# The down product of a gated FFN: eleven pairs by seven products instead of nine pairs and a plain rest

## The chip, the core and the metric

The kernel runs on one core of one Trainium2 chip. The core has a matrix engine (TensorE, "PE" in the profile, its weight loads "PEld"), a vector engine (VectorE, "DVE"), a scalar engine (ScalarE, "ACT"), a general engine (GpSimd, "POOL") and a queue engine (SyncE, "SP") that issues most DMAs; the engines run at the same time and wait for each other by semaphores. The metric is the time of one execution in microseconds (us) on the device.

## The reference

The program is a two-layer decoder trunk on 512 tokens of width 1024, all in float32. Layer 0 has a state-space mixer, layer 1 multi-head latent attention; each is followed by a layer norm, a gated FFN and a second layer norm. The change concerns the FFN:

```python
def conv_ffn(h, up, conv_w, conv_b, down):
    u = causal_depthwise_conv(h @ up, conv_w, conv_b)
    g, val = jnp.split(u, 2, axis=-1)
    return (jax.nn.silu(g) * val) @ down
...
ff = conv_ffn(h, ffn_up[i], ffn_conv_w[i], ffn_conv_b[i], ffn_down[i])
h = layer_norm(DN_ALPHA * h + ff, ln_ffn_g[i], ln_ffn_b[i])
```

The hidden width is 2816, which is 22 hidden tiles of 128. FFN 0 is followed by the attention's down projection, FFN 1 by the output.

## The kernel before, in words

**Precision.** Every float32 operand of a product is split into a high part (rounded to the matmul format by ACT) and a low part (the difference, by DVE). A product is three matmuls: high times high, high times low, low times high (`mm_b`). One matmul has a 128x128 stationary tile and 512 moving columns.

**The weight stream (`WStream`).** All weights of the program are a list of items in the order of use. `load` brings an item into a staging tile `wst` (SP's queue), `_split` makes its high and low parts `wh` and `wl` (ACT line 96, DVE line 97). There are six buffers of `wh` and of `wl`; `ahead` splits items until these are taken, `retire` gives a pair back when the last product has used it. Items have a kind: "r" loads into a running sum `rs`, "a" adds onto that sum by a DMA that accumulates (POOL's queue), "+" adds a staged tile onto the sum on DVE (line 88), "=" is that staged tile itself, "-" is the sum minus a staged tile (DVE, line 91), no kind is a plain weight.

**An FFN.** In an up phase, each hidden tile takes two items (gate and value, 24 matmuls each, line 159), and `conv3_silu_gate` makes the gated tile on ACT and DVE (lines 327 to 333). Two hidden tiles make a pair: `pair_operands` builds from the even and odd tile, cut in two halves of 256 tokens, the seven left operands of a seven-multiplication scheme for 2x2 blocks (Winograd's form of Strassen's), named a11, a12, a22, s1, s2, s3, s4, and splits them into `gt` buffers (18 of them). a11 needs the even tile alone. The right operands are the sums and differences that the item kinds make, and the results are added onto the residual stream `h` by DVE (line 387). A round is an up phase and then the seven products of its pairs; the pairs are grouped into parts of two or one (a part of two has weight items of 1024 columns).

Before the change there are two rounds, with parts (2,2,1) and (2,1,1), which is nine pairs or 18 hidden tiles, and the last four hidden tiles (their up items come in the second round's up phase, after its pairs') are multiplied plainly after the second round: for each token tile of 128 both halves of 512 columns, 24 matmuls in all (`piece`, lines 165 to 167), then that tile's layer norm. `add_mix` (line 185) adds with a row sum, `ln_stats` takes the mean on DVE and the squares on ACT, `ln_var` the factor on DVE or POOL, `ln_a` (line 210) and `ln_b` (line 215) are two DVE passes of two halves. In FFN 0 the finished tiles are transposed on TensorE for the attention (`transpose_h`, lines 274 to 278), tiles 0 and 1 inside the tail and tiles 2 and 3 inside the attention's start; in FFN 1 they are written out, and the last token tile is cut in two halves of 256 columns (`ln_last`, lines 243 to 264).

**What sets the order.** A framework orders each engine's queue at build time: of the instructions whose inputs it takes to be ready, the earliest in program order goes first. So an instruction can stand in its queue well ahead of its place in the program. `issue_after(x)` ties the instructions of a block behind x on x's engine. SP's queue is ordered by hand. On the chip each engine's queue runs in that fixed order.

Of the kernel before, what the change touches and what calls it, by code (L numbers as in the profile page):

```python
# [18 lines left out]
P = 128  # L19
# [11 lines left out]
class WStream:  # L31
# [44 lines left out]
    def _split(self, nst=None):  # L76
# [17 lines left out]
        h = self.k.wh.tile([P, 1024], F32R, name="wh")  # L94
        l = self.k.wl.tile([P, 1024], F32R, name="wl")
# [16 lines left out]
    def retire(self, i):  # L112
        assert i == self.done
        del self.w[i]
        self.done += 1


class K:
# [87 lines left out]
    def ln_a(self, i, dst):  # L206

        for f in range(2):
            sl = slice(f * 512, (f + 1) * 512)
            self.nc.vector.scalar_tensor_tensor(dst[:, sl], self.h[:, i, sl], self.st[i][:, 2:3], self.gb[0][:, sl],  # L210
                                                op0=ALU.add, op1=ALU.mult)

    def ln_b(self, i, f, src):
        sl = slice(f * 512, (f + 1) * 512)
        self.ln_end = self.nc.vector.scalar_tensor_tensor(self.h[:, i, sl], src[:, sl], self.st[i][:, 5:6], self.gb[1][:, sl],
# [15 lines left out]
    def ln_last(self, i, bs, out, between):  # L231
# [19 lines left out]
        nc.vector.scalar_tensor_tensor(h3, h3, 1.0, bs[1], op0=ALU.mult, op1=ALU.add, accum_out=sb)  # L251
# [14 lines left out]
    def transpose_h(self, i):  # L266
# [3 lines left out]
        for q in range(2):  # L270
# [7 lines left out]
            nc.vector.tensor_tensor(self.htt[:, q * 4:(q + 1) * 4, 1, ts], bv, hi, op=ALU.subtract)  # L278
# [9 lines left out]
RP0 = ((2, 2, 1), (2, 1, 1))  # L288
RP1 = ((2, 2, 1), (2, 1, 1))


def rounds(rp):
    r0 = 2 * sum(rp[0])
    return r0, r0 + 2 * sum(rp[1])


def ffn_items(up, down, rp):
# [4 lines left out]
    R0, R1 = rounds(rp)  # L302
    dv = down.rearrange("(k p) n -> p k n", p=P)
    for r, ks in enumerate((range(R0), range(R0, HT))):
        for c in ks:
            it.append((up[c], 1024))
            it.append((up[c + HT], 1024))

        for odd, hf, kinds in ((0, 0, "r"), (0, 1, "a"), (1, 1, "+="), (0, 0, "-"), (1, 0, None), (1, 0, "a")):
            j = ks[0]  # L310
            for p, n in enumerate(rp[r]):
                b = dv[:, j:j + 2 * n, hf * 512:(hf + 1) * 512].rearrange("p (k e) n -> p k e n", e=2)[:, :, odd, :]
                it += [(b, n * 512, kind, p) for kind in kinds or (None,)]
# [47 lines left out]
def down_pairs(k, ws, n, prs, parts, first, between):  # L361

    nc = k.nc
    X, Y, Z = ([k.bank() for _ in range(2)] for _ in range(3))
    ni = len(parts)
    at = [sum(parts[:p]) for p in range(ni + 1)]
    new = {(i, hf) for i in range(NT) for hf in range(2)} if first else set()  # L370

    def product(bs, op, p, i, start, stop):
        wh, wl = ws.get(i, 3)
        ps = prs[at[p]:at[p + 1]]
        for t in range(2):
            for q, pr in enumerate(ps):
                x, c0 = pr[op]
                sl = slice(q * 512, (q + 1) * 512)
                k.mm_b(bs[t], x, slice(c0 + t * P, c0 + (t + 1) * P), wh[:, sl], wl[:, sl],
                       start and p == 0 and q == 0, stop and p == ni - 1 and q == len(ps) - 1)  # L380
        ws.retire(i)

    def add(bs, row, hf, sign):
        for t in range(2):
            i = 2 * row + t
            hs = k.h[:, i, hf * 512:(hf + 1) * 512]
            last = nc.vector.scalar_tensor_tensor(hs, hs, ALPHA if (i, hf) in new else 1.0, bs[t], op0=ALU.mult,  # L387
                                                  op1=ALU.add if sign > 0 else ALU.subtract)
            new.discard((i, hf))
        return last  # L390

    def ahead(n, ins):

        with k.tc.issue_after(ins.ins):
            ws.ahead(n)

    for p in range(ni):
        product(X, "a11", p, n + p, True, True)
    n += ni
    ahead(n, add(X, 0, 0, 1))  # L400
    for p in range(ni):
        product(Y, "s1", p, n + p, True, True)
    n += ni
    ahead(n, add(Y, 1, 1, 1))
    between()
    for p in range(ni):
        product(X, "s2", p, n + 2 * p, False, True)
        product(Y, "s4", p, n + 2 * p + 1, False, True)
    n += 2 * ni
    add(X, 0, 1, -1)  # L410
    ahead(n, add(Y, 0, 1, 1))
    for bs, op, s0, out in ((X, "s3", False, (1, 1, -1)), (Z, "a12", True, (0, 0, 1)), (X, "a22", False, (1, 0, 1))):
        for p in range(ni):
            product(bs, op, p, n + p, s0, True)
        n += ni
        ahead(n, add(bs, *out))
    return n


def ffn(k, ws, base, cwp, gb, rp, la=2, out=None, mid=None):  # L420

    nc, tc = k.nc, k.tc
    R0, R1 = rounds(rp)
    with ExitStack() as c:
        pool = lambda n, b: c.enter_context(tc.tile_pool(name=n, bufs=b))
        pools = {"gt": pool("gt", 18), "fw": pool("fw", 7), "rs": pool("rs", 1), "cw": pool("cw", 1)}
# [18 lines left out]
        for r in range(2):  # L445
            gts, prs = [], []
# [19 lines left out]
            c0 = r * R0  # L466
# [21 lines left out]
            for ci in range(c0, HT if r else R0):  # L488
# [15 lines left out]
        nk = HT - R1
        nw = nk // 2

        def piece(i, b, hf, c0, c1, retire):
            for jc in range(nw):
                wh, wl = ws.get(n + hf * nw + jc)
                for jj in range(2):  # L510
                    j = jc * 2 + jj
                    o = slice(jj * 512 + c0, jj * 512 + c1)
                    k.mm_b(b, gts[j], slice(i * P, (i + 1) * P), wh[:, o], wl[:, o], j == 0, j == nk - 1)
                if retire:
                    ws.retire(n + hf * nw + jc)

        xn = {}
# [961 lines left out]
```

## Time and profile before

| | |
|---|---|
| Median of 3 runs | 1307.0 us (1306.98 to 1307.31) |
| The profiled execution | 1306.91 us, span 1305.2 us, clock of TensorE 0.998 |
| TensorE busy | 1296.5 us in 6570 matmuls |
| DVE, ACT, POOL busy | 1008.0, 630.7, 67.5 us |
| FFN 0: up phase 2, products of round 2, plain tail | 577.6, 708.1, 746.2 to 768.6 us |
| FFN 1: products of round 1, of round 2, plain tail | 1059.2, 1237.7, 1275.7 to 1297.5 us |

The span is the time from the first to the last instruction of the profiled execution; its own time is 1.7 us longer. A group's row in the profile reads: line, engine, operation, tiles and shapes, count | busy us, mean ns of one | idle time of the engine just before, and what ended it. A timeline's row reads: start us, length us, engine, line, operation.

### The profile page before, as it was taken

The page shows a single profiled execution, that of the slowest core. Times are in us where ns is not written, and L with a number is a line of the kernel's source. Part 1 is how long each engine was busy: PE and PEld are TensorE (multiplying, and loading weights), DVE is VectorE, ACT ScalarE, POOL GpSimd, SP SyncE. Part 2 cuts the span into 40 slices and gives each one's busy share as a digit, 9 for nine tenths or more (in the row PEclk, how much of TensorE's full clock was granted, in tenths as well). Part 3 has the DMA queues.
Part 4 walks back from the last instruction along what each step waited for, and adds up shares of the span by engine and source line. Part 5 has one row for each costly group of instructions (what it writes and reads, how often), then busy time and mean ns, then how long its engine had stood idle before and what let it go on. Part 6 is the DMA issues. An engine that isn't in the chain of part 4 may idle for free.

```text
span 1305.2 us, 17262 instructions
## 1 busy us (share of the span) xinstructions
PE 1296.5 (99%) x6570; PEld 1100.7 (84%) x6570; DVE 1008.0 (77%) x1605; ACT 630.7 (48%) x1022; POOL 67.5 (5%) x88
## 2 busy tenths in 40 slices
PE   9999999999999999999999999999999999999997
PEld 8888888888888988888888899888898888888886
DVE  7788888787799868866766876898587786667587
ACT  6766545536533544444443434665254444444341
POOL 0000000000001001100000012000100000000000
PEclk9999999999999999999999999999999999999999
DMA  8533323324411433352312721231054226333251
GB/s 298 192 125 114 142 101 102 131 73 144 161 62 68 130 129 81 76 206 95 126 63 33 249 89 61 70 109 49 17 180 137 69 40 208 129 97 105 41 162 64
DMA packets 52082, 147.72 MB, mean 113 GB/s; under 512 B 5568, under 2 KB 8640, under 8 KB 50720
## 3 DMA queue, kind: packets, MB, share of 16 engines
q1 hardware_dynamic: 46784, 136.71, 30.5%
q0 software_dynamic: 5072, 9.77, 4.4%
q8 instruction: 51, 0.84, 0.3%
q14 instruction: 31, 0.25, 0.1%
q10 hardware_dynamic: 144, 0.15, 0.0%
HBM read 144.44 MB, written 2.16 MB: 112 GB/s over the span
## 4 chain that ended last, share of the span: by engine, by line
PE 99%; DVE 0%; issue 0%; ACT 0%; DVEq 0%; ACTq 0%
PE ps L159 58%; PE ps L165 10%; PE ps L167 10%; PE ps L166 10%; PE ps L1276 2%; PE ps L800 1%; PE ps L1317 1%; PE ps L925 1%; PE ps L274 1%; PE ps L816 1%; PE ps L1299 1%; PE ps L789 1%; PE ps L743 1%; PE ps L767 1%; PE ps L620 0%; PE ps L838 0%
## 5 line engine op out<-in xcount | busy, mean ns | idle before, releaser
L159 PE MATMUL ps<-ht,wh 128*128 128x512 f32 (+1 forms) x2256 | 517.1, 379 | 0.0
L159 PEld LDWEIGHTS ps<-ht,wh 128*128 128x128 f32 x2256 | 408.1, 188 | 79.6 <-issue 1.4
L97 DVE TENSOR_TENSOR wl<-wst,wh 128x1024 fp32r<-128x1024 f32 (+3 forms) x222 | 253.4, 1158 | 39.8 <-ACT wh L96 38.7
L96 ACT CAST wh<-wst 128x1024 fp32r<-128x1024 f32 (+3 forms) x222 | 218.7, 995 | 125.3 <-PE ps L167 68.5
L159 PE MATMUL ps<-ht,wl 128*128 128x512 f32 (+1 forms) x1128 | 266.7, 379 | 0.0
L159 PEld LDWEIGHTS ps<-ht,wl 128*128 128x128 f32 x1128 | 205.2, 188 | 39.7
L328 DVE SCALAR_TENSOR_TENSOR acc<-ps,cw,acc 128x511 f32<-128x511 f32 x88 | 65.7, 747 | 80.1 <-ACT acc L327 80.1
L165 PE MATMUL ps<-wh,gt 128*128 128x512 f32 (+1 forms) x320 | 123.7, 387 | 0.0
L167 PE MATMUL ps<-wh,gt 128*128 128x512 f32 (+1 forms) x320 | 123.6, 386 | 0.0
L166 PE MATMUL ps<-wl,gt 128*128 128x512 f32 (+1 forms) x320 | 123.6, 386 | 0.0
L340 ACT CAST gt<-acc 128x512 fp32r<-128x512 f32 (+1 forms) x80 | 44.0, 571 | 101.9 <-DVE acc L333 99.3
L327 ACT ACTIVATE acc<-ps,cw 128x512 f32<-128x512 f32 x88 | 68.3, 776 | 29.5 <-PE ps L159 29.4
L658 DVE SCALAR_TENSOR_TENSOR cv<-ps,cw,cv 128x511 f32<-128x511 f32 (+2 forms) x72 | 53.7, 745 | 21.7 <-ACT cv L656 21.1
L166 PEld LDWEIGHTS ps<-wl,gt 128*128 128x128 f32 x320 | 60.1, 188 | 12.2
L165 PEld LDWEIGHTS ps<-wh,gt 128*128 128x128 f32 x320 | 60.1, 188 | 12.2
L167 PEld LDWEIGHTS ps<-wh,gt 128*128 128x128 f32 x320 | 60.1, 188 | 12.1
L332 ACT ACTIVATE acc<-acc 128x512 f32<-128x512 f32 x44 | 27.8, 632 | 87.6 <-DVE acc L329 87.4
L329 DVE SCALAR_TENSOR_TENSOR acc<-ps,cw,acc 128x510 f32<-128x510 f32 x88 | 65.8, 747 | 2.5
L96 ACT CAST wh<-rs 128x1024 fp32r<-128x1024 f32 (+1 forms) x48 | 39.9, 834 | 46.1 <-DVE rs L88 27.1
L341 DVE TENSOR_TENSOR gt<-acc,gt 128x512 fp32r<-128x512 f32 (+1 forms) x80 | 48.7, 627 | 13.5 <-ACT gt L340 13.5
L387 DVE SCALAR_TENSOR_TENSOR h<-h,ps 128x512 f32<-128x512 f32 x56 | 37.5, 685 | 25.6 <-PE ps L167 25.6
L52 POOL DMA_DIRECT2D rs<-in_down_dram x24 | 25.1, 1045 | 576.1 <-DVE wl L97 576.1
(248 smaller groups left out, 1727.2 us busy)
## 6 DMA issues: line engine op xcount, KB each, us to landing
wst<-in_up_dram SPq DMA_DIRECT2D x88, 512.0 KB, 3.5
wst<-in_xbc_dram SPq DMA_DIRECT2D x32, 512.0 KB, 6.3
wst<-in_down_dram SPq DMA_DIRECT2D x26, 512.0 KB, 5.8
W<-cumd SPq DMA_DIRECT2D x8, 1024.0 KB, 4.7
wst<-in_sow_dram SPq DMA_DIRECT2D x16, 512.0 KB, 3.5
wst<-in_zw_dram SPq DMA_DIRECT2D x14, 512.0 KB, 6.0
rs<-in_down_dram POOLq DMA_DIRECT2D x12, 512.0 KB, 6.9
wst<-in_down_dram SPq DMA_DIRECT2D x18, 256.0 KB, 2.6
```

Of the source, the lines that this page charges most:

```text
L96: nc.scalar.copy(h[:, :f], s[:, :f])
L97: nc.vector.tensor_tensor(l[:, :f], s[:, :f], h[:, :f], op=ALU.subtract)
L159: nc.tensor.matmul(out, w[:, k, :], xts[k][:, x, ts], start=first and p == 0 and k == 0, stop=last and p == 2 and k == nk - 1, skip_group_ ...
L165: nc.tensor.matmul(out, xt[:, 0, tsl], wh, start=start, stop=False, skip_group_check=True)
L166: nc.tensor.matmul(out, xt[:, 0, tsl], wl, start=False, stop=False, skip_group_check=True)
L167: nc.tensor.matmul(out, xt[:, 1, tsl], wh, start=False, stop=stop, skip_group_check=True)
L327: nc.scalar.activation(a, b, AF.Identity, bias=cw[:, ch, 3:4], scale=cw[:, ch, 2:3])
L328: nc.vector.scalar_tensor_tensor(a[:, 1:], b[:, :SEQ - 1], cw[:, ch, 1:2], a[:, 1:], op0=ALU.mult, op1=ALU.add)
L329: nc.vector.scalar_tensor_tensor(a[:, 2:], b[:, :SEQ - 2], cw[:, ch, 0:1], a[:, 2:], op0=ALU.mult, op1=ALU.add)
L340: k.nc.scalar.copy(dst[:, 0, :], src)
L341: k.nc.vector.tensor_tensor(dst[:, 1, :], src, dst[:, 0, :], op=ALU.subtract)
L658: nc.vector.scalar_tensor_tensor(t[:, d:], b[:, :SEQ - d], cw[:, ch, 3 - d:4 - d], t[:, d:], op0=ALU.mult, op1=ALU.add)
```

## The change

Three rounds with parts (2,2), (2,1), (2,2) take all 22 hidden tiles; the plain rest is gone. `down_pairs` becomes the class `Pairs` with `start` (a11 and s1) and `rest`. Now s1 of a part follows a11 of that part at once, so items are retired out of order (`gone`).

The first two rounds use `start` and `rest`. The last round uses `start` with the two column halves exchanged, and then goes by token tiles: a12 for tiles 0 and 1, then s2 and s4 for tile 0, s2 and s4 for tile 1, s3 and a22 for tile 2, s3 and a22 for tile 3, each tile's layer norm after its last product. Its items come in another order (`LAST`): the plain weight a12 ahead of the sum and difference, and these part by part. The "-" items of the last round do not take `wh` and `wl` buffers but two `gt` buffers each ("own", `apart`). The norm's parameters are loaded after hidden tile 19 of the up phase. `ln_a` writes into two `acc` tiles instead of a `gt` row; in FFN 0 the norms of tiles 2 and 3 stand at the very end, and the attention's first weights are split in three steps tied behind the squares and the transposed halves. In `ln_last` the add of the last 256 columns is tied behind `dist`.

```diff
@@ class WStream
+    def apart(self, i):
+        return len(self.items[i]) > 4
...
-        h = self.k.wh.tile([P, 1024], F32R, name="wh")
-        l = self.k.wl.tile([P, 1024], F32R, name="wl")
+        if self.apart(i):
+            h, l = self.own(), self.own()
+        else:
+            h = self.k.wh.tile([P, 1024], F32R, name="wh")
+            l = self.k.wl.tile([P, 1024], F32R, name="wl")
...
-        lim = min(len(self.items), i + (self.la if la is None else la) + 1, self.done + self.nb, self.split + most)
-        while self.split < lim:
+        lim = min(len(self.items), i + (self.la if la is None else la) + 1, self.split + most)
+        while self.split < lim and (self.apart(self.split) or self.room()):
             self._split()
+    def room(self):
+        return sum(not self.apart(j) for j in range(self.done, self.split)) < self.nb
@@ def ln_last
-        nc.vector.scalar_tensor_tensor(h3, h3, 1.0, bs[1], op0=ALU.mult, op1=ALU.add, accum_out=sb)
+        with self.tc.issue_after(dist.ins):
+            nc.vector.scalar_tensor_tensor(h3, h3, 1.0, bs[1], op0=ALU.mult, op1=ALU.add, accum_out=sb)
@@
-RP0 = ((2, 2, 1), (2, 1, 1))
-RP1 = ((2, 2, 1), (2, 1, 1))
+RP = ((2, 2), (2, 1), (2, 2))
...
+R, SUM, MIX, DIF, RAW = (0, 0, "r"), (0, 1, "a"), (1, 1, "+="), (0, 0, "-"), (1, 0, None)
+FIRST = ((R,), (SUM,), (MIX,), (DIF,), (RAW,), ((1, 0, "a"),))
+LAST = ((R,), (SUM,), (RAW,), (MIX, DIF), ((1, 0, "a"),))
@@ class Pairs
+    def start(self, f):
+        X, Y, ni = self.X, self.Y, self.ni
+        for p in range(ni):
+            self.product(X, "a11", p, self.n + p, True)
+            if p == ni - 1:
+                a = self.adds(X, 0, f, 1)
+                with self.k.tc.issue_after(a.ins):
+                    self.ws.ahead(self.n + 2 * ni - 1)
+            self.product(Y, "s1", p, self.n + ni + p, True)
+        self.n += 2 * ni
+        self.ahead(self.adds(Y, 1, 1 - f, 1))
@@ def ffn, the last round
+        pp = Pairs(k, ws, n, prs, rp[-1], False)
+        pp.start(1)
+        pp.la = 0
...
+        ws.ahead(end - 1, 0)
...
+        for t in range(2):
+            one_tile(pp.Z[t:], "a12", t, True)
+            pp.add(pp.Z[t], t, 1, 1, True)
+        ws.ahead(end - 1, 0)
+        for t in range(2):
+            one_tile(pp.X[t:], "s2", t, False)
+            a = pp.add(pp.X[t], t, 0, -1)
+            if t:
+                with tc.issue_after(a.ins):
+                    ln_bs(0)
+            one_tile(pp.Y[t:], "s4", t, False)
+            a = pp.add(pp.Y[t], t, 0, 1, True)
+            if out is None:
+                stats(t)
+            if not t:
+                ln_a(t)
+        with tc.issue_after(a.ins):
+            ws.ahead(end - 1, 0)
+            ln_a(1)
+            if out is None:
+                with tc.issue_after(k.ln_sq.ins):
+                    ws.ahead(end, 1)
+        for t in range(2):
+            i = 2 + t
+            one_tile(pp.X[t:], "s3", t, False)
+            pp.add(pp.X[t], i, 0, -1, True)
+            a = pp.add(pp.X[t], i, 1, 1)
+            with tc.issue_after(a.ins):
+                if not t:
+                    ln_bs(1)
+                elif out is not None:
+                    ln_b(2, 0)
+            cuts = ((0, 256), (256, 512)) if t and out is not None else ((0, 512),)
+            bs = [k.bank()[:, :c1 - c0] for c0, c1 in cuts]
+            one_tile(bs, "a22", t, True, cuts)
+            if len(bs) > 1:
+                k.ln_last(i, bs, out[i * P:(i + 1) * P, :], lambda: ln_b(2, 1))
+                continue
+            a = pp.add(bs[0], i, 1, 1, True)
+            if out is not None:
+                ln_a(i)
+                continue
+            sq = k.ln_sq
+            stats(i)
+            with tc.issue_after(a.ins):
+                k.transpose_h(t)
+            with tc.issue_after(k.ht_end.ins), tc.issue_after(sq.ins):
+                ws.ahead(end, la if t else 3)
+        if out is None:
+            for i in (2, 3):
+                ln_a(i)
+                ln_bs(i)
```

More of the change, by code (lines that the diff above doesn't have):

```diff
@@ L43, in __init__ @@
         self.w = {}
+        self.gone = set()
+        self.own = None
+    def apart(self, i):
+        return len(self.items[i]) > 4
     def load(self, i):
@@ L112, in retire @@
     def retire(self, i):
-        assert i == self.done
         del self.w[i]
-        self.done += 1
+        if self.apart(i):
+            return
+        self.gone.add(i)
+        while self.done in self.gone:
+            self.gone.remove(self.done)
+            self.done += 1
+            while self.done < len(self.items) and self.apart(self.done) and self.done not in self.gone:
+                self.gone.add(self.done)
 class K:
@@ L358, in pair_operands @@
     split(k, s34, v)
[L361 to L374, printed above, removed]
-        for t in range(2):
[L376 to L383, printed above, removed]
-        for t in range(2):
[L385 to L412, printed above, removed]
-        for p in range(ni):
[L414 to L417, printed above, removed]
@@ L434, in ffn @@
         rs = k.lnp.tile([P, 2, DM], F32, name="rs", tag="lngb")
-        ws.sums = [rs[:, 0], rs[:, 1], pools["rs"].tile([P, 512], F32, name="rs2")]
+        ws.sums = [rs[:, 0], rs[:, 1]]
         new_gt = lambda: pools["gt"].tile([P, 2, SEQ], F32R, name="gt")
+        ws.own = lambda: new_gt().rearrange("p a n -> p (a n)")
         row = lambda nm: pools["gt"].tile([P, DM], F32, name=nm, tag="gt")
@@ L487, in ffn @@
                 c0 += 2
-            for ci in range(c0, HT if r else R0):
+            for ci in range(c0, at[r + 1]):
                 bg, bv = k.bank(), k.bank()
@@ L497, in ffn, with stats, ln_a @@
                 finish(ci, bg, bv)
+                if ci == HT - 3:
+                    norm_params()
             if mid and not r:
                 mid()
-            n = down_pairs(k, ws, n, prs, rp[r], not r, norm_params if r else lambda: None)
+            if r < len(rp) - 1:
+                pp = Pairs(k, ws, n, prs, rp[r], not r)
+                pp.start(0)
+                n = pp.rest()
         if out is None:
             k.new_ht()
[L504 to L515, printed above, removed]
-        xn = {}
+        xn = {}
+        def stats(i):
+            m = k.ln_stats(i)
+            if out is None:
+                k.ln_var(i, nc.gpsimd)
+            return m
+        def ln_a(i):
+            xn[i] = [pools["fw"].tile([P, SEQ], F32, name="acc") for _ in range(2)]
+            if out is not None:
+                stats(i)
+            a = k.ln_a(i, xn[i])
+            if out is not None:
+                k.ln_var(i, nc.vector)
+            return a
         def ln_b(i, f):
@@ new lines, in ffn, with one_tile @@
+        pp = Pairs(k, ws, n, prs, rp[-1], False)
+        ni = pp.ni
+        pp.start(1)
+        pp.la = 0
+        end = pp.n + 5 * ni
+        at = {"a12": (0, 1), "s2": (ni, 3), "s4": (ni + 1, 3), "s3": (ni + 2, 3), "a22": (4 * ni, 1)}
+        ws.ahead(end - 1, 0)
+        def one_tile(bs, op, t, start, cuts=((0, 512),)):
+            a, d = at[op]
+            for b, (c0, c1) in zip(bs, cuts):
+                for p in range(ni):
+                    pp.tile(b, op, p, pp.n + a + d * p, t, start, c0, c1)
+                    if t and c1 == 512:
+                        ws.retire(pp.n + a + d * p)
@@ L556, in ffn @@
         if out is None:
-            for f in range(2):
-                ln_b(NT - 1, f)
-        n += 2 * nw
+            for i in (2, 3):
+                ln_a(i)
+                ln_bs(i)
+        n = end
     ws.nst = 3
```

143 lines of the change are left out of this document (85 added, 58 removed).

## The prediction

> **What bounds the kernel now.** I read the page first: its busy times and the shares of the chain that ended last.
>
> ```profile
> span 1305.2 us, 17262 instructions
> ...
> PE 1296.5 (99%) x6570; PEld 1100.7 (84%) x6570; DVE 1008.0 (77%) x1605; ACT 630.7 (48%) x1022; POOL 67.5 (5%) x88
> ...
> PE 99%; DVE 0%; issue 0%; ACT 0%; DVEq 0%; ACTq 0%
> ```
>
> TensorE is busy 1296.5 of 1305.2 us and carries the chain. The 8.7 us without it lie at the two ends. So a matmul that disappears is worth its pace, as long as nothing makes TensorE wait. Next, the chain in order of time (columns: start, length, what): it gives the pace, the hand-over from FFN 0 to the attention, and the end.
>
> ```profile
> 577.55 130.56 PE ps L159 x576
> ...
> 768.85 0.87 PE ps L274 x8
> 777.44 0.87 PE ps L274 x8
> ...
> 1296.18 0.44 DVE h L243 x2
> ...
> 1301.56 0.40 DVE h L263
> ```
>
> 576 matmuls of 512 columns take 130.56 us, 0.2267 us each (a "mean" of 390 ns in other views is a matmul's latency; they overlap). Third, the busy times in five stretches: product round 2 and the plain tail of FFN 0, product round 1 of FFN 1, then its round 2 and its plain tail.
>
> ```profile
> 708.12:746.20 38.08, 38.08 (x169) 31.54 (x169) 31.03 (x40) 17.96 (x23) 2.96 (x3) 1.00 0.59 184
> 746.20:768.60 22.40, 22.40 (x104) 18.64 (x104) 19.36 (x36) 8.59 (x12) 2.65 (x6) 1.00 0.26 88
> 1059.20:1107.00 47.80, 47.80 (x213) 39.59 (x212) 37.00 (x47) 21.64 (x26) 3.25 (x3) 1.00 0.50 144
> 1237.70:1275.70 38.00, 38.00 (x169) 31.50 (x168) 31.04 (x40) 16.85 (x22) 2.94 (x3) 1.00 0.47 139
> 1275.70:1297.50 21.80, 21.80 (x108) 18.41 (x107) 16.35 (x40) 4.15 (x7) 1.66 (x3) 1.00 0.15 57
> ```
>
> Columns: PE, weight loads, DVE, ACT and POOL busy, clock, DMA. PE is full in all five. DVE follows at 75 to 86%, and that is the number to watch: the change moves work onto it.
>
> **Removed: matmuls.** Two hidden tiles cost 2 x 4 token tiles x 2 halves x 3 = 48 matmuls plainly, and 7 x 2 x 3 = 42 by seven products. Two pairs per FFN change sides, two FFNs: 24 matmuls, 24 x 0.2267 = **-5.44 us**. The other rounds only regroup (5+4 pairs become 4+3+4).
>
> **Added: DVE work.** Durations of one, by shape:
>
> ```profile
> L97 DVE TENSOR_TENSOR wl<-wst,wh 128x1024 fp32r<-128x1024 f32 x191 | 229.9, 1218 | 35.1 <-ACT wh L96 34.2 <-DMA wst<-in_down_dram 0.8
> ...
> L387 DVE SCALAR_TENSOR_TENSOR h<-h,ps 128x512 f32<-128x512 f32 x56 | 37.5, 685 | 25.6 <-PE ps L167 25.6
> ...
> L278 DVE TENSOR_TENSOR ht<-ps,ht 128x512 fp32r<-128x512 f32 x24 | 15.4, 682 | 1.9 <-ACT ht L277 1.6
> ...
> L210 DVE SCALAR_TENSOR_TENSOR xn<-h,lnst,lng 128x512 f32<-128x512 f32 x14 | 10.0, 749 | 0.2
> ...
> L91 DVE TENSOR_TENSOR wst<-rs,wst 128x1024 f32<-128x1024 f32 x6 | 7.3, 1222 | 0.1
> L88 DVE TENSOR_TENSOR rs<-rs,wst 128x1024 f32<-128x1024 f32 x6 | 7.3, 1218 | 0.0
> ```
>
> In a queue they overlap a little: in the timeline at the end of FFN 0's first up phase (below) two splits start 1.14 us apart, so I count 1.14 for 1024 columns and 0.65 for 512.
>
> ```profile
> 527.44 1.22 DVE L88 TENSOR_TENSOR rs<-rs,wst 128x1024 f32<-128x1024 f32 x1
> 528.57 0.74 DVE L329 SCALAR_TENSOR_TENSOR acc<-ps,cw,acc 128x510 f32<-128x510 f32 x1
> 529.23 1.22 DVE L91 TENSOR_TENSOR wst<-rs,wst 128x1024 f32<-128x1024 f32 x1
> ...
> 529.79 0.39 PE L165 MATMUL ps<-wh,gt 128*128 128x512 f32 x1
> ...
> 530.81 0.75 DVE L328 SCALAR_TENSOR_TENSOR acc<-ps,cw,acc 128x511 f32<-128x511 f32 x1 [0.36 <-ACT acc L327]
> ...
> 535.96 1.29 DVE L341 TENSOR_TENSOR gt<-acc,gt 128x512 fp32r<-128x512 f32 x2 [0.23 <-ACT gt L340]
> 537.17 1.28 DVE L387 SCALAR_TENSOR_TENSOR h<-h,ps 128x512 f32<-128x512 f32 x2
> ...
> 541.90 1.22 DVE L97 TENSOR_TENSOR wl<-wst,wh 128x1024 fp32r<-128x1024 f32 x1
> 543.04 1.21 DVE L97 TENSOR_TENSOR wl<-rs,wh 128x1024 fp32r<-128x1024 f32 x1
> ```
>
> Now the new last round. Call 0 the moment its first product starts (here 529.8). TensorE runs pieces of 12 matmuls, 2.72 us: a11 and s1 alternating by part until 10.9, a12 until 16.3, then s2/s4 of tile 0 (from 16.3) and of tile 1 (21.8), s3/a22 of tile 2 (27.2) and of tile 3 (32.6), end 38.1. That spaces the finished token tiles by 5.44 us, just as the plain tail does: tile 0 is done 16.3 us before the end in both.
>
> DVE must do in these 38.1 us, in FFN 1: the last up tile and pair operands, 530.81 to 537.17 less one split, 5.8; splits after 0: one of a12 1.1, s2/s4/s3 of the first part 5 x 1.14 = 5.7, of the second part 3.4 if its sum and difference (L88, L91) run during the up phase, two of a22 2.3; sixteen adds 10.4; layer norm of tiles 0 to 2, four passes of 0.67 and small ones, 9.0. **37.7 of 38.1 us**, where old round 2 and tail had 31.04 + 16.35 in 59.8. FFN 0 adds two transposed tiles (4 x 0.65) and six attention weights (four of 1024 columns, two of 768: 6.3) and may leave tile 2's norm (2.7) for later: 43.9. DVE, with some 2 us of unavoidable waits, is as full as TensorE here; what it delivers late decides what is left of 5.44.
>
> **Does TensorE wait inside the round?** I walked the queues through with these durations. The first part's s2 weights stand behind the adds of a11 (issue_after), about 9.6; sum 1.14, cast, two splits, and s2 is ready at 14.3 against 16.3. The second part's are needed at 17.7 and ready by 11 if L88 was pulled forward, as above, where L88 and L91 of a later part ran at 527.44 and 529.23, before the products began. s3 is ready at 21.5 (needed 27.2). The a22 sums come over POOL's queue:
>
> ```profile
> rs<-in_down_dram POOLq DMA_DIRECT2D x12, 512.0 KB, 6.9
> ```
>
> Issued at 18 after the difference, landed at 25, split by 27.2, needed at 29.9. Cost **0**; the cover is 1.5 to 6 us each. In the middle round (2,1) the last pair's s1 is needed at 6.8, and L341 above shows it written 6.8 after the products began (529.8 to 536.6), half a microsecond ahead of the third matmul that wants the low half: 0, between 0 and 0.6 a round.
>
> The two norm-parameter loads move from between s1 and s2 of the old round 2 into the last up phase; they need two gt buffers, of which 7 of 18 are free then, and delay the queue behind them by their issue time, about half a microsecond each (row below). First use is tile 0's norm, 30 us on: 0.
>
> ```profile
> 721.76 0.47 SPq L443 DMA_DIRECT2D lng<-in_gb_dram  x1
> ```
>
> **The end of FFN 1.** Rows of DVE, and the last matmul of the first 256-column half:
>
> ```profile
> 1294.75 0.69 DVE L185 SCALAR_TENSOR_TENSOR h<-h,ps 128x512 f32<-128x512 f32 x1 [0.25 <-PE ps L167]
> ...
> 1295.36 0.75 DVE L215 SCALAR_TENSOR_TENSOR h<-xn,lnst,lnb 128x512 f32<-128x512 f32 x1
> 1296.18 0.42 DVE L243 SCALAR_TENSOR_TENSOR h<-h,ps 128x256 f32<-128x256 f32 x1
> ```
>
> ```profile
> 1295.86 0.28 PE L167 MATMUL ps<-wh,gt 128*128 128x256 f32 x1
> ```
>
> L243 starts just as its half is ready, and everything after it is a chain of 9.0 us to the end of the span. After the change the stretch between s3 of tile 3 (ready 35.6) and L243 (ready 37.0) holds two adds instead of one, then L215: 35.6 + 1.3 + 0.7 = 37.6. **+0.6 us**, from 0 (the order puts L215 later) to 1.5 (every DVE duration 4% longer, by the same walk).
>
> **The hand-over of FFN 0.** Before, DVE was already behind there:
>
> ```profile
> 769.26 2.95 DVE L97 TENSOR_TENSOR wl<-wst,wh 128x1024 fp32r<-128x1024 f32 x3
> ...
> 772.74 1.28 DVE L278 TENSOR_TENSOR ht<-ps,ht 128x512 fp32r<-128x512 f32 x2
> ```
>
> The sixth attention weight was ready at 772.2, TensorE's transposes ended at 769.7, and a token tile of that projection takes 7.7 us (769.72 to 777.44), so the fifth and sixth weights are wanted 5.6 and 6.7 us after its start: 3 to 4 us to spare. After, these two splits follow tile 1's transposed halves on DVE and end, by my walk, at 47.9 and 48.7, where the projection starts at 39.9 and wants them at 45.5 and 46.6. That is 2.1 to 2.4 late; if DVE leaves tile 2's norm until after them (2.7), 0. Both orders satisfy the code; I take the middle, **+1.2**, from 0 to 3.5 (2.4 plus the same 4% on 28 us of queue).
>
> One rule speaks against a fuller DVE. POOL's power step took 0.56 us beside a waiting DVE and 0.98 beside a busy one:
>
> ```profile
> 754.32 0.56 POOL L204 TENSOR_TENSOR lnst<-lnst,mhalf 128x1 f32<-128x1 f32 x1
> ...
> 765.57 0.98 POOL L204 TENSOR_TENSOR lnst<-lnst,mhalf 128x1 f32<-128x1 f32 x1
> ```
>
> The Trainium skill, SBUF — State Buffer, "Who interferes with whom", says that a DVE instruction with two SBUF inputs contends with a GpSimd instruction that reads SBUF; the trace agrees with its 0.42 us. By it, three norms of the last round get their factor 0.4 later each; L215 waits for none of them in my walk, so the sum would not move.
>
> **Sum**, against the profiled execution's own 1306.9: 1306.9 - 5.4 + 0.6 + 1.2 = 1303.3. The median of the runs is 0.1 higher: **1303.4**.
>
> **Rivals.**
> *All hidden* (L215 and the late splits fall into DVE's gaps): 1307.0 - 5.4 = 1301.6. For it: before, none of these places cost TensorE anything. Against: 37.7 of 38.1 has no gaps. 0.07.
> *A draw*: DVE falls behind by 3 to 4 us in FFN 0 (the upper bound 3.5) and the end slips by 1.5, with 0.6 in each middle round: -5.4 + 3.5 + 1.5 + 1.2 = +0.8, 1307.8; anything from 2.8 us of waits on counts here. For it: DVE's share; against: before, 5.3 us of lateness at the hand-over (768.6 to 773.95) cost TensorE nothing. 0.25.
> *Slower: the second part's sum and difference are not pulled forward.* Then both stand on DVE behind the adds of s1, s2 of tile 0 waits 2.35 us in either FFN (walked: 1.28 and 1.07), and the 2.4 us of extra queue come out again at the ends: L243 3.9 late in place of 0.6, the attention's start 3.9 late in all; with the middle rounds' 0.6 each, 1307.0 - 5.4 + 3.9 + 3.9 + 1.2 = 1310.6. It decides once L88 of the second part runs after 12. For it: the code ties neighbours of these splits behind adds; against: the rows at 527.44 and 529.23. 0.15, with other mishaps of that size.
> The skill's TensorE: Matmul & The Clock Gate, "HAM oscillation", has idle gaps above 3.4 us halve the clock. No single wait here reaches that, and no run here shows it in mid-kernel.
>
> **How the numbers follow.** Forecast 0.53, all hidden 0.07, draw 0.25, slower 0.15. What a measurement of this kernel can tell from no change is about 0.2%, 2.6 us: faster means below 1304.4. Forecast and all-hidden lie there, 0.60; same 0.25; slower, above 1309.6, 0.15. The forecast's own range is 1301.9 to 1304.4. The range for 8 in 10 starts under the full gain, 1301.2, and takes in the draw up to 1308.0.
>
> **What would show it.** 24 fewer matmuls at a 0.227 pace; L88 of the second part before the last round's first product; no gap on TensorE before s2 of tile 0; a gap of 0 to 2.4 us in the first attention tile, ended by a split L97; L243's counterpart about half a microsecond after its bank is ready. I am wrong if TensorE has gaps elsewhere in the down rounds, or if the attention starts without any and the end slips by more than 2.

## The result and the profile after

The changed kernel takes 1313.9 us (median of 6 runs, 1313.3 to 1315.0) against 1307.3 (6 runs, 1307.0 to 1308.5) for the kernel before: a ratio of 1.005, with a 95% interval of 1.0037 to 1.0063. It is slower by 0.5%, where 0.3% faster was forecast. The profiled execution took 1314.98 us, 1.7 more than its span; it is the slowest of the six, 1.1 above their median.

The page of the kernel after, busy times and the shares of the chain that ended last:

```profile
span 1313.3 us, 17205 instructions
...
PE 1295.7 (99%) x6546; PEld 1097.4 (84%) x6546; DVE 1032.9 (79%) x1637; ACT 636.2 (48%) x1022; POOL 72.0 (5%) x88
...
PE 88%; issue 6%; DVE 3%; DMA 1%; ACT 0%; POOL 0%; DVEq 0%; ACTq 0%; POOLq 0%
```

The 24 matmuls are gone (6570 to 6546), but the chain is no longer TensorE alone: 3% of it is DVE and 1% is a DMA ("issue" is time on the chain in which an engine waited for nothing that the profile shows). What TensorE waited for stands in the view of waits (who waits, for whom, us in total, times, longest):

```profile
PE ps L184 <- DVE h L422: 4.1, 1, 4.1
...
PE ps L296 <- DVE h L236: 0.4, 1, 0.4
```

In the kernel after, line 94 is the "+" add, 97 the "-", 105 and 106 the two halves of a split, 422 the add onto `h`, 184 to 186 a product's matmuls, 264 the add of the last tile's first 256 columns. The timeline shows the last round of FFN 0 (its first product starts at 727.81), here with the rows of DVE, ACT, POOL and TensorE picked out and put together:

```profile
721.26 1.22 DVE L94 TENSOR_TENSOR rs<-rs,wst 128x1024 f32<-128x1024 f32 x1
722.74 1.22 DVE L97 TENSOR_TENSOR wst<-rs,wst 128x1024 f32<-128x1024 f32 x1
...
743.58 2.42 POOL L58 DMA_DIRECT2D rs<-in_down_dram  x2 [32.28 <-issue]
...
749.41 1.05 ACT L105 CAST wh<-rs 128x1024 fp32r<-128x1024 f32 x1 [4.39 <-DMA rs<-in_down_dram]
756.19 1.04 ACT L105 CAST wh<-rs 128x1024 fp32r<-128x1024 f32 x1 [5.73 <-DMA rs<-in_down_dram]
...
750.49 1.23 DVE L106 TENSOR_TENSOR wl<-rs,wh 128x1024 fp32r<-128x1024 f32 x1 [1.75 <-ACT wh L105]
757.26 1.23 DVE L106 TENSOR_TENSOR wl<-rs,wh 128x1024 fp32r<-128x1024 f32 x1 [5.55 <-ACT wh L105]
758.41 1.47 DVE L422 SCALAR_TENSOR_TENSOR h<-h,ps 128x512 f32<-128x512 f32 x2
...
754.78 0.39 PE L186 MATMUL ps<-wh,gt 128*128 128x512 f32 x1
759.23 0.77 PE L184 MATMUL ps<-gt 128*128 128x512 f32 x1 [4.06 <-DVE h L422]
759.80 0.63 PE L185 MATMUL ps<-gt 128*128 128x512 f32 x1
...
764.06 0.63 PE L186 MATMUL ps<-gt 128*128 128x512 f32 x1
...
764.87 0.39 PE L185 MATMUL ps<-wl,gt 128*128 128x512 f32 x1
```

Read it from the end. TensorE stops after 754.78 and goes on at 759.23 with s3 of tile 2, which adds into the bank that holds s2 of tile 0. That bank must first be read by the add at 758.41. The add didn't wait for TensorE: it stood in DVE's queue behind the two splits of the a22 weights (750.49 and 757.26), and these waited for ACT's casts, and the casts for the two accumulating loads, which POOL issued at 743.58. The second landed at about 756.1. Then comes a second loss: from 759.23 to 764.87 there are 13 starts in 5.64 us, where 0.2267 each gives 2.95. TensorE runs at about half pace and loses another 2.7 us, and the granted clock of that stretch shows it (columns as in the prediction's windows):

```profile
754.90:764.50 9.60, 5.54 (x15) 4.14 (x14) 6.25 (x11) 2.29 (x3) 0.74 (x2) 0.66 0.03 9
```

In FFN 1 the same two splits stand in the same place (DVE's rows, then the first add of the last tile and the last matmul):

```profile
1285.57 1.23 DVE L106 TENSOR_TENSOR wl<-rs,wh 128x1024 fp32r<-128x1024 f32 x1 [1.76 <-ACT wh L105]
1288.19 1.23 DVE L106 TENSOR_TENSOR wl<-rs,wh 128x1024 fp32r<-128x1024 f32 x1 [1.39 <-ACT wh L105]
1289.33 1.47 DVE L422 SCALAR_TENSOR_TENSOR h<-h,ps 128x512 f32<-128x512 f32 x2
...
1304.25 0.41 DVE L264 SCALAR_TENSOR_TENSOR h<-h,ps 128x256 f32<-128x256 f32 x1
...
1301.19 0.28 PE L186 MATMUL ps<-wh,gt 128*128 128x256 f32 x1
```

Here the loads land earlier and TensorE waits for almost nothing, but DVE never catches up: L264 runs 3.1 us after the last matmul has started, where its counterpart before (L243 at 1296.18, last matmul 1297.30) ran 1.1 ahead of it. The end is 4.2 us longer.

Two numbers split every run in its two FFNs: where FFN 1's first up phase starts in the chain (before, 955.42; the row of after is below), and the rest of the span.

```profile
961.24 82.25 PE ps L178 x408
```

| | up to FFN 1 | rest | span |
|---|---|---|---|
| before | 955.4 | 349.8 | 1305.2 |
| forecast (-2.7 + 1.2; -2.7 + 0.6) | 953.9 | 347.7 | 1301.6 |
| after | 961.2 | 352.1 | 1313.3 |

So of the 11.7 us of span that the forecast missed (10.5 by the medians), 7.3 are lost in FFN 0 (4.06 + 2.7 are the wait and the half pace) and 4.4 in FFN 1, 3.6 of these at its end (4.2 against 0.6).

### The profile page after: what moved, and what is told of

Same layout as the page of the kernel before. It is cut to its first block, busy times and chain, and to the rows that moved or that the text cites. A ratio compares the mean times of both kernels' runs of the same rounds, so it can differ in the third digit from the quotient of the medians.

```text
span 1313.3 us, 17205 instructions
## 1 busy us (share of the span) xinstructions
PE 1295.7 (99%) x6546; PEld 1097.4 (84%) x6546; DVE 1032.9 (79%) x1637; ACT 636.2 (48%) x1022; POOL 72.0 (5%) x88
## 4 chain that ended last, share of the span: by engine, by line
PE 88%; issue 6%; DVE 3%; DMA 1%; ACT 0%; POOL 0%; DVEq 0%; ACTq 0%; POOLq 0%
PE ps L178 55%; PE ps L185 8%; PE ps L186 8%; PE ps L184 7%; PE ps L1364 2%; DMA rs<-in_down_dram 1%; PE ps L888 1%; PE ps L1405 1%; PE ps L1013 1%; DVE wl L106 1%; PE ps L904 1%; DVE h L422 1%; PE ps L296 1%; PE ps L1387 1%; PE ps L877 1%
## 5 line engine op out<-in xcount | busy, mean ns | idle before, releaser
L106 DVE TENSOR_TENSOR wl<-wst,wh 128x1024 fp32r<-128x1024 f32 (+3 forms) x210 | 245.4, 1185 | 36.6 <-ACT wh L105 36.4
L105 ACT CAST wh<-wst 128x1024 fp32r<-128x1024 f32 (+3 forms) x210 | 209.4, 1015 | 110.9 <-PE ps L186 52.2
L185 PE MATMUL ps<-wl,gt 128*128 128x512 f32 (+1 forms) x296 | 114.6, 387 | 0.2
L186 PE MATMUL ps<-wh,gt 128*128 128x512 f32 (+1 forms) x296 | 114.2, 387 | 0.0
L184 PE MATMUL ps<-wh,gt 128*128 128x512 f32 (+1 forms) x296 | 113.6, 387 | 0.0
L370 ACT CAST gt<-acc 128x256 fp32r<-128x256 f32 (+1 forms) x88 | 47.8, 566 | 106.8 <-DVE acc L363 97.5
L106 DVE TENSOR_TENSOR wl<-rs,wh 128x1024 fp32r<-128x1024 f32 (+1 forms) x48 | 54.4, 1133 | 32.3 <-ACT wh L105 32.2
L105 ACT CAST wh<-rs 128x1024 fp32r<-128x1024 f32 (+1 forms) x48 | 46.7, 977 | 66.4 <-DMA rs<-in_down_dram 34.8
L185 PEld LDWEIGHTS ps<-wl,gt 128*128 128x128 f32 x296 | 55.7, 188 | 12.2 <-DVE wl L106 1.1
L184 PEld LDWEIGHTS ps<-wh,gt 128*128 128x128 f32 x296 | 55.7, 188 | 11.8 <-ACT gt L370 0.4
L186 PEld LDWEIGHTS ps<-wh,gt 128*128 128x128 f32 x296 | 55.4, 188 | 11.6 <-DVE gt L371 0.5
L422 DVE SCALAR_TENSOR_TENSOR h<-h,ps 128x512 f32<-128x512 f32 x87 | 56.7, 681 | 6.8 <-PE ps L186 6.4
```

The lines of the kernel that those rows point to most:

```text
L105: nc.scalar.copy(h[:, :f], s[:, :f])
L106: nc.vector.tensor_tensor(l[:, :f], s[:, :f], h[:, :f], op=ALU.subtract)
L184: nc.tensor.matmul(out, xt[:, 0, tsl], wh, start=start, stop=False, skip_group_check=True)
L185: nc.tensor.matmul(out, xt[:, 0, tsl], wl, start=False, stop=False, skip_group_check=True)
L186: nc.tensor.matmul(out, xt[:, 1, tsl], wh, start=False, stop=stop, skip_group_check=True)
L370: k.nc.scalar.copy(dst[:, 0, :], src)
```

## The experiments

Three theories. **Order:** the a22 splits stand too early in DVE's queue, ahead of the adds of s2. **Landing:** the sums themselves come too late, whatever the order; and in FFN 0 later than in FFN 1, because six attention weights are loaded beside them. **Volume:** DVE has too much work in the last round, and the wait would turn up in some other place.

**e_tie_late**: the untied call goes.

```diff
             one_tile(pp.Z[t:], "a12", t, True)
             pp.add(pp.Z[t], t, 1, 1, True)
-        ws.ahead(end - 1, 0)
```

> Edit: the second, untied call that looks ahead for the a22 weights goes away; their two splits are written down only behind the s4 add of token tile 1, where a call for them stands already. Same instructions, another place in DVE's and ScalarE's queues. Order theory (the splits stand ahead of tile 0's s2 add and hold it until the accumulating loads have landed): the wait of 4.06 us on TensorE ahead of s3 of tile 2 in FFN 0 goes, and with it the half clock behind it (2.4), together -6.5; in FFN 1 DVE isn't held up and the first half of the last tile is added within 1 us of its bank, -3 to -4. Total 1303 to 1305. Volume theory (DVE simply has too much work in the last round, wherever it stands): 1312 to 1315, the idle time turns up in another place.

Measured: 1312.7 us, 1.0041 of before (1.0026 to 1.0056). The order theory alone missed by 8 us, and the volume theory's 1312 to 1315 came true; e_noacc and e_hold_tie below decide against it. Its timeline (ACT, DVE, TensorE):

```profile
755.91 1.05 ACT L105 CAST wh<-rs 128x1024 fp32r<-128x1024 f32 x1 [5.66 <-DMA rs<-in_down_dram]
756.87 1.15 ACT L213 ACTIVATE lnjunk<-h,lnst 128x1024 bf16<-128x1024 f32 x1
...
759.07 1.41 DVE L236 SCALAR_TENSOR_TENSOR h<-acc,lnst,lnb 128x512 f32<-128x512 f32 x2 [6.17 <-POOL lnst L223]
...
762.28 0.80 PE L185 MATMUL ps<-wl,gt 128*128 128x512 f32 x1 [4.44 <-DVE wl L106]
```

The add is free now, but the late load holds ACT instead: its cast stands ahead of tile 0's squares (L213), the norm's factor on POOL waits for the squares, DVE waits 6.17 us for the factor, and the split behind that makes TensorE wait 4.44 us for a22. The stall moved by one engine.

**e_tie**: the same call, tied behind the s4 add of tile 0.

```diff
-        ws.ahead(end - 1, 0)
...
             if not t:
+                with tc.issue_after(a.ins):
+                    ws.ahead(end - 1, 0)
                 ln_a(t)
```

> Edit: the same two splits behind the s4 add of token tile 0, 5.4 us earlier than in e_tie_late. Order theory: the add that TensorE waited for in FFN 0 (s2 of tile 0) is now ahead of the splits, so that wait goes, -4 to -6.5; but the second load of FFN 0 still lands only at about 756, and DVE still stands behind it, now with tile 1's adds: the lateness stays in DVE's queue, up to 1 us of it reaches TensorE before a22 of tile 2, and in FFN 1 the end is better by 1 to 3 only. Total 1305 to 1309, between after and e_tie_late. Volume theory: 1312 to 1315, and no different from e_tie_late.

Measured: 1310.2 us, 1.0024 (1.0015 to 1.0034). Better than expected of volume, a little worse than the order theory had it. The wait ahead of s3 is gone, and so is the half clock (1.00 in the stretch where after has 0.66), but DVE still stands 5.40 us ahead of the second split, with tile 0's norm and tile 1's adds behind it. FFN 1 starts at 958.5.

**e_noacc**: the load takes no sum (the other terms of the a22 sum are left out).

```diff
-LAST = ((R,), (SUM,), (RAW,), (MIX, DIF), ((1, 0, "a"),))
+LAST = ((R,), (SUM,), (RAW,), (MIX, DIF), ((1, 0, None),))
```

> Edit: in the last round the a22 weights come by one plain load each on SyncE's queue into the stage of weights in place of accumulating loads over POOL's queue; the splits stand as untied and as early as in after. Left out: the other terms of the a22 sum, so the down product is not the reference's. DVE has the same instructions in the same order. Order theory: the weights are there long before, the splits don't wait, no wait ahead of s3 in FFN 0, no lateness at the end of FFN 1: 1302 to 1305. Volume theory: DVE's work is unchanged, 1312 to 1315.

Measured: 1304.1 us, 0.9978 (0.9968 to 0.9988). With the splits as early and as untied as in after, and DVE's instructions the same, all of the loss goes. So the place in the queue hurts only because the weights aren't there. The splits no longer wait (both in 2.36 us, no idle time ahead of them):

```profile
748.31 2.36 DVE L106 TENSOR_TENSOR wl<-wst,wh 128x1024 fp32r<-128x1024 f32 x2
```

**e_more**: six more loads at the end of FFN 1.

```diff
         items += ffn_items(d['up'][1], d['down'][1], RP)
+        items += [(d['up'][1][j], 1024) for j in range(6)]
```

> Edit: after, and six more loads of 512 KB behind the last round of FFN 1, of the size and at the place in the queue of the six attention weights behind FFN 0; nothing reads them. It asks why the second accumulating load took 11.6 us from issue to landing in FFN 0 and 7.5 in FFN 1. Contention theory (the attention's loads slow it): the second landing in FFN 1 goes from 7.5 to 10 to 12 us, DVE's idle time ahead of the second split from 1.4 to about 5, TensorE waits 2 to 4 us ahead of s3 of tile 2 in FFN 1 too and runs at half pace for some time behind it: total +3 to +7 on after, 1317 to 1321. Against it: the landing stays at 7 to 8 us and the total within 1 us of after; then FFN 0's 11.6 has another cause.

Measured: 1314.3 us, 1.0054 (1.0039 to 1.0069), as after; the second landing of FFN 1 stayed at 7.2 us. But this tested nothing: SP's and POOL's rows show that the extra loads had gone out before the accumulating loads were issued, since their staging tiles were free earlier than in FFN 0.

```profile
1262.65 3.85 SPq L60 DMA_DIRECT2D wst<-in_up_dram  x3
1269.32 1.56 SPq L60 DMA_DIRECT2D wst<-in_up_dram  x2
...
1277.76 2.42 POOL L58 DMA_DIRECT2D rs<-in_down_dram  x2 [32.30 <-DVE wst L97]
```

**e_hold**: the other way round, FFN 0's own loads are held back.

```diff
-        for i in range(self.split, min(len(self.items), self.split + self.nb + self.nst)):
+        for i in range(self.split, min(len(self.items), self.split + self.nb + self.nst, self.stop)):
...
+        if out is None:
+            ws.stop = n + 7 * ni + 2
         pp.start(1)
...
+        if out is None:
+            for p in range(2):
+                nc.sync.dma_start(pools["fw"].tile([P, SEQ], F32, name="acc")[:, :1], ws.sums[p][:, :1])
+            ws.stop = 1 << 30
         ws.ahead(end - 1, 0)
```

> Edit: after, with the last four of the six attention weights of FFN 0 held back in SyncE's queue until both accumulating loads of its last round have landed (two loads of 4 bytes a partition out of the sums stand ahead of them and wait). It asks again why the second accumulating load took 11.6 us in FFN 0. Contention theory: the second landing of FFN 0 comes down from 11.6 to 7 to 8 us, as in FFN 1, the wait ahead of s3 of tile 2 from 4.06 to under 0.7 us and the half clock behind it goes, -5 to -6.5: 1307 to 1309.5; FFN 1 stays as in after. Against it: landing 11 to 12 us, 1313 to 1315.

Measured: 1310.1 us, 1.0026 (1.0016 to 1.0036), a little less gain than expected. ACT's casts show the landings (where an edit adds lines, the line numbers move by one or more: ACT's half of a split is L106 here):

```profile
750.55 1.05 ACT L106 CAST wh<-rs 128x1024 fp32r<-128x1024 f32 x1 [4.55 <-DMA rs<-in_down_dram]
753.16 1.05 ACT L106 CAST wh<-rs 128x1024 fp32r<-128x1024 f32 x1 [1.56 <-DMA rs<-in_down_dram]
```

The second weight follows the first by 2.6 us, as in FFN 1; in after (749.41, 756.19) it was 6.8. From issue to landing it took 7.6 us in place of 11.6. So the attention's loads beside it made the difference. The wait ahead of s3 is gone; FFN 1 is as long as in after (351.8 against 352.1).

**e_tie2 and e_hold_tie**: part 0's splits behind the s4 add of tile 0, part 1's behind the s2 add of tile 1; e_hold_tie holds the last three attention weights back as well.

```diff
-        ws.ahead(end - 1, 0)
         for t in range(2):
             one_tile(pp.X[t:], "s2", t, False)
             a = pp.add(pp.X[t], t, 0, -1)
             if t:
                 with tc.issue_after(a.ins):
+                    ws.ahead(end - 1, 0)
                     ln_bs(0)
...
             if not t:
+                with tc.issue_after(a.ins):
+                    ws.ahead(end - 2, 0)
                 ln_a(t)
```

> Edit: both repairs that leave DVE's work as it is: the last three attention weights of FFN 0 held back until the accumulating loads have landed (e_hold), and the splits tied, part 0's behind the s4 add of tile 0, part 1's behind the s2 add of tile 1. If e_hold's and e_tie's gains are separate causes (late landing in FFN 0, place in the queue), they join: FFN 0 within 1 us of its time in e_noacc, FFN 1 1 to 2.5 us behind it: 1305 to 1308. If they are one cause, no better than the better of them, 1310.

> Edit: e_hold_tie without its hold: part 0's a22 splits behind the s4 add of tile 0, part 1's behind the s2 add of tile 1, the six attention weights loaded as in after. It is the fourth corner of a square with after, e_hold and e_hold_tie. Two causes (place in the queue in both FFNs, late landing in FFN 0 by the attention's loads): the second load of FFN 0 lands at about 756 again, DVE stands idle there 3 to 5 us with tile 0's norm and tile 1's s4 add behind it, the hand-over to the attention is 2.5 to 4 us later than in e_hold_tie; FFN 1 as in e_hold_tie (first half of the last tile added within 0.7 us of its bank). Total 1307.3 to 1309. If the order alone had been enough: 1304.8 to 1305.5. If the hold is all: 1310 or more.

Measured: e_hold_tie 1304.8 us, 0.9982 (0.9973 to 0.9991), faster than both kernels and a little better than expected of two causes. e_tie2 1308.2 us, 1.0006 (0.9997 to 1.0015), inside the range expected of two causes. The square, as start of FFN 1 and rest of the span:

| | loads as in after | loads held back |
|---|---|---|
| splits untied | after: 961.2, 352.1 | e_hold: 958.2, 351.8 |
| splits tied | e_tie2: 957.3, 349.4 | e_hold_tie: 953.9, 349.2 |

The hold is worth 3.0 and 3.4 us, and in FFN 0 alone. The tie is worth 3.9 to 4.3 in FFN 0 and 2.6 to 2.7 in FFN 1. They are two causes and nearly add up. The square holds profiled executions, and those of after and e_hold lie 1.1 and 1.6 us above the medians of their runs; by the medians the hold is worth 3.8 and 3.3 us in all, the tie 5.7 and 5.3, so a size read from the square can be 1 to 1.6 us off. DVE's rows of e_tie2, and below them those of e_hold_tie:

```profile
756.90 1.23 DVE L106 TENSOR_TENSOR wl<-rs,wh 128x1024 fp32r<-128x1024 f32 x1 [3.19 <-ACT wh L105]
```

```profile
749.74 0.69 DVE L423 SCALAR_TENSOR_TENSOR h<-h,ps 128x512 f32<-128x512 f32 x1 [0.43 <-PE ps L187]
...
750.36 1.22 DVE L107 TENSOR_TENSOR wl<-rs,wh 128x1024 fp32r<-128x1024 f32 x1
...
753.67 1.22 DVE L107 TENSOR_TENSOR wl<-rs,wh 128x1024 fp32r<-128x1024 f32 x1
```

In e_hold_tie the splits find their weights ready and DVE waits for TensorE's s4 instead (0.43). The windows of its two last rounds, FFN 0's and FFN 1's:

```profile
727.80:765.90 38.10, 38.10 (x174) 31.64 (x173) 35.35 (x55) 18.97 (x24) 4.29 (x6) 1.00 0.42 112
1255.70:1293.80 38.10, 38.10 (x181) 31.99 (x179) 35.16 (x60) 15.13 (x19) 4.08 (x5) 1.00 0.24 56
```

TensorE is full in both and DVE is busy 35.2 to 35.4 of 38.1 us: it fits. Its page has DVE at 1033.0 us in 1637 instructions, as in after (1032.9), and the run is 9 us faster. That ends the volume theory as the cause.

**e_pool, e_pool_tie, e_dveadd, e_dveadd_tie, e_mix_tie**: other ways to the same sum. The a22 weight comes early by a plain load, and POOL or DVE adds the sum to it; "tie" puts the splits behind the s4 add of tile 0; e_mix_tie does this on DVE for part 0 alone and lets part 1 accumulate.

```diff
-LAST = ((R,), (SUM,), (RAW,), (MIX, DIF), ((1, 0, "a"),))
+LAST = ((R,), (SUM,), (RAW,), (MIX, DIF), ((1, 0, "p"),))
...
+        elif kind == "p":
+            nc.gpsimd.tensor_tensor(s[:, :f], self.sums[part][:, :f], s[:, :f], op=ALU.add)
```

(nc.vector in e_dveadd, e_dveadd_tie and e_mix_tie.)

> Edit: after, but the a22 weights of the last round come by a plain load each over SyncE's queue, early, and GpSimd adds the sum to them (2 adds of 128x1024 per FFN; its 128x512 tensor_tensor took 1.42 us, so 2.8 each); the result is the reference's. The splits stand untied as in after. Landing theory (the accumulating load comes back too late for the place of its split, in either FFN; DVE itself has room): as e_noacc, 1303 to 1305.5, if GpSimd beside DVE costs nothing much. Volume theory (e_noacc was fast because the sum was missing) would have 1309 or more.

> Edit: e_pool with the a22 splits tied behind the s4 add of tile 0 as in e_tie. If only the landing mattered, the place of the splits is worth nothing once the weights are there: within 1 us of e_pool. If the place matters by itself (two splits of 1.14 us each ahead of the s2 add of tile 0): 0.5 to 2 us below e_pool.

> Edit: as e_pool, but DVE makes the two adds of each FFN (1.22 us a piece in the trace, 2.3 in the queue). It doubles as a test of DVE's fullness: the last round then holds 2.3 us more DVE work than after. Landing theory with room on DVE: 1303.5 to 1306. If DVE is as full as the sum of the prediction had it (37.7 of 38.1 us): each FFN ends 1.9 to 2.3 later than in e_pool, 1307 to 1310.

> Edit: e_dveadd with adds and splits of the a22 weights tied behind the s4 add of tile 0. No accumulating load is left behind the first products, so what is measured is DVE's room: two adds of 1.14 more than after, in a place where nothing waits at once. Place matters little once the weights are there (e_pool_tie took 1.0 off e_pool): 1306 to 1307.4; if DVE has room, 1304 to 1306.

> Edit: of the two a22 weights of the last round, part 0 (wanted first) comes by a plain load and an add on DVE, part 1 by the accumulating load as in after, alone now; part 0's splits are tied behind the s4 add of tile 0, part 1's behind the s2 add of tile 1. The result is the reference's. Landing theory: the one accumulating load lands in 5 to 6 us (FFN 1) and 6 to 9 (FFN 0), ahead of its place in the queue in FFN 1 and about there in FFN 0; DVE has 1.14 more a round. No wait on TensorE above 1 us, the end of FFN 1 0.5 to 1.5 behind its bank: 1304.5 to 1306.5. If a fuller DVE is what counts (as e_dveadd's 1307.4 can be read): 1306 to 1308.

| | median us | of before (95%) | up to FFN 1 | rest |
|---|---|---|---|---|
| e_pool | 1307.5 | 1.0005 (0.9996 to 1.0014) | 955.4 | 350.4 |
| e_pool_tie | 1306.5 | 0.9996 (0.9987 to 1.0006) | 954.6 | 350.3 |
| e_dveadd | 1307.4 | 1.0002 (0.9992 to 1.0011) | 955.3 | 350.4 |
| e_dveadd_tie | 1307.7 | 1.0005 (0.9996 to 1.0014) | 955.5 | 350.1 |
| e_mix_tie | 1307.6 | 1.0002 (0.9993 to 1.0011) | 955.2 | 350.3 |

All five take the late landing away and come back to the time before, 1.7 to 2.9 us above e_hold_tie. e_pool fell between its two forecasts; e_dveadd and e_mix_tie came out on the side of a full DVE, and e_dveadd_tie 0.3 above its range; e_pool_tie, 1.0 below e_pool, fits both of its readings. For POOL the reason is in the rows (of e_pool_tie): while its add runs, a split on DVE takes twice its time.

```profile
739.10 2.42 POOL L99 TENSOR_TENSOR wst<-rs,wst 128x1024 f32<-128x1024 f32 x1 [1.17 <-DVE rs L94]
740.20 2.40 DVE L108 TENSOR_TENSOR wl<-rs,wh 128x1024 fp32r<-128x1024 f32 x1
...
742.52 1.21 DVE L108 TENSOR_TENSOR wl<-wst,wh 128x1024 fp32r<-128x1024 f32 x1
```

So each of the five puts a microsecond or more onto DVE in each round, and against e_hold_tie time is lost: 0.6 to 1.5 us up to the start of FFN 1 and 1.0 to 1.3 in the rest. Up to FFN 1 the loss of the three runs with DVE adds is what TensorE waits for DVE at the hand-over, in e_mix_tie for tile 2's norm and for a split of an attention weight:

```profile
PE ps L298 <- DVE h L238: 0.7, 1, 0.7
PE ps L187 <- DVE wl L108: 0.6, 1, 0.6
```

e_hold_tie has neither wait. In e_dveadd and e_dveadd_tie the same two take 1.3 and 1.6 us; in the POOL runs the waits for DVE are shorter (1.1 us in e_pool, 0.3 in e_pool_tie) and cover half of the loss or more. In the rest the loss stands at the end again: the add of the last tile's first 256 columns starts 1.6 us behind the last matmul in e_mix_tie and e_dveadd_tie and 1.1 to 1.3 in the POOL runs, where e_hold_tie has 0.5. So DVE has room for what after asks of it and for little more. One DVE add (e_mix_tie) costs nearly as much as two (e_dveadd_tie), and DVE's rows suggest why: in e_mix_tie DVE stands 0.76 us ahead of tile 1's s2 add, waiting for TensorE, and in e_dveadd_tie the second add of 1.14 us fills that gap.

```profile
752.10 0.69 DVE L426 SCALAR_TENSOR_TENSOR h<-h,ps 128x512 f32<-128x512 f32 x1 [0.76 <-PE ps L188]
```

## Why the prediction was wrong

**The step that failed** is the one on the a22 sums in "Does TensorE wait inside the round?": "Issued at 18 after the difference, landed at 25, split by 27.2, needed at 29.9. Cost 0". Issue came earlier than that (743.58, or 15.8 after the first product), and the first weight landed at 21.6. Two things were wrong.

*The landing of the second.* The walk took the median of a group, 6.9 us, for both. In FFN 0 it was 11.6, cast at 28.4 and split by 30.7. A median of twelve loads of the kernel before hides what was loaded beside each; the attention's weights stood in the same part of the prediction, as work for DVE, but not as traffic. e_hold and e_hold_tie show the effect: 3.0 and 3.4 us. By itself the late landing would hardly have been late for TensorE: a22 of tile 2 uses the second part only after six matmuls of the first, at 31.3 by the prediction's walk. It cost what it did through DVE's queue.

*What stands behind the waiting splits.* The walk asked when the split was needed and not where it stands. The untied call behind the a12 loop (line 598 of the kernel after) lets the framework put both splits straight behind the adds of a12, ahead of the s2 add of tile 0, so even the early landing in FFN 1 held up the adds. e_tie2 and e_hold_tie show this: 3.9 to 4.3 us in FFN 0, 2.6 to 2.7 in FFN 1.

**The clock.** "No single wait here reaches that" failed with it. The wait of 4.06 us was followed by 13 starts at about half pace. The Trainium skill, TensorE: Matmul & The Clock Gate, "HAM oscillation", has gaps above about 3.4 us halve the clock; the runs agree, since waits of 3.63 (e_more), 4.06 and 4.44 us (e_tie_late) were followed by slow matmuls, and one of 1.5 us (e_tie) was not. By themselves the runs put the bound only between 1.5 and 3.6 us.

**The other terms**, read from e_hold_tie, where the failed step is mended. The 24 matmuls are real, and so is FFN 0's total: 953.92 measured, 953.9 forecast, though from other parts: 0.45 in the middle round, about 0.4 at tile 2's transposes (775.52), beside the norm's last pass on DVE (774.63), and some 0.35 that no single row accounts for. The middle round cost nearly 0.45 us in each FFN and not 0, inside the 0 to 0.6 given: two matmuls fewer start in the same stretch. The windows of the kernel before and, below, of the kernel after:

```profile
600.00:650.00 50.00, 50.00 (x222) 41.40 (x222) 36.92 (x54) 23.63 (x34) 0.00 (x0) 1.00 0.31 101
```

```profile
600.00:650.00 50.00, 49.92 (x220) 40.68 (x219) 40.54 (x55) 21.57 (x28) 2.12 (x2) 1.00 0.46 143
```

Most of the 0.45 doesn't stand where the prediction looked, at the last pair's operands, but ahead of a matmul that reads a weight's low half, behind the splits of DVE (the chain of after):

```profile
626.94 1.83 DVE wl L106 x2
628.82 0.50 PE ps L185
```

The hand-over did not cost 1.2 in the way that was walked: no gap in the first attention tile ends with a split, in after or in e_hold_tie. But the late attention splits, which the +1.2 rested on, are real where DVE is a little later: in e_tie, e_tie2 and e_hold one such gap of 1.5 us stands there, and in the runs with DVE adds one of 0.6 to 0.9. The waits of e_tie2:

```profile
PE ps L185 <- DVE wl L106: 1.5, 1, 1.5
...
PE ps L296 <- DVE h L236: 0.7, 1, 0.7
```

The end of FFN 1 was sized too low, at +0.6:

```profile
1294.20 0.41 DVE L265 SCALAR_TENSOR_TENSOR h<-h,ps 128x256 f32<-128x256 f32 x1
...
1293.70 0.28 PE L187 MATMUL ps<-wh,gt 128*128 128x256 f32 x1
```

This counterpart of L243 stands 0.5 behind the last matmul, where before it stood 1.1 ahead: +1.6, a little past the upper bound of 1.5. The fullness of DVE was seen rightly, 35.2 busy of 38.1 with the waits that the prediction set aside, and the waits for DVE in the five runs with more DVE work show that little room is left. One reading was off, at no cost to the sum: POOL's power step of 0.56 us ran for the most part beside DVE's add out of a bank (754.39), not beside a waiting DVE.

**The rivals.** "Slower" came true, but not by its mechanism: the second part's sum and difference (721.26, 722.74) ran ahead of the first product, as the forecast said, so that its 1310.6 lies near by accident. The mechanism that decided was in none of the cases; the prediction's own warning, gaps elsewhere in the down rounds, is what happened. With the step mended, e_hold_tie's 1304.8 is 1.4 us above the forecast of 1303.4.

## What to carry to other kernels

For each instruction that a change lets run early, ask two things: what lands last for it, and what stands behind it in the same queue until then; an early place is free only if its inputs are there. Where a load's time comes from a group's median, look at what else is being loaded in the stretch in which the new one will run. A mended wait can come back one engine further on (e_tie_late), so look at every queue that the late input passes through.

## What the runs showed of the hardware

A 512 KB accumulating load took 5.4 to 5.9 us from issue to landing as the first of two, 7.1 to 7.6 as the second with nothing else beside it (FFN 1) or the attention's loads held back (FFN 0 of e_hold and e_hold_tie), and 11.2 to 11.6 as the second beside loads of the attention's weights. Alone of its kind (e_mix_tie) it took 5.5 us in FFN 1 and 8.3 in FFN 0, beside those loads. Plain loads of that size have medians of 3.5 to 6.5 us in the view of DMAs of the kernel after.

POOL's 128x1024 add took 2.42 us, and a DVE split that started inside it 2.40 in place of 1.21. The Trainium skill, SBUF — State Buffer, "Who interferes with whom", has a DVE instruction with two SBUF inputs contend with a GpSimd instruction that reads SBUF; the rows agree.
